# Two 512-column and 256-column matmuls in place of three 256-column ones in five weight products of a hybrid block

## The chip, the cores and the metric

One core of one Trainium2 chip runs the whole kernel. The metric is the device time of one execution in microseconds, as the median of several runs; smaller is better.

## The reference

Two transformer-like blocks run one after the other on 256 tokens of width 1024 (float32). Cut to what matters here:

```python
# block 1
proj = rms_norm(x, norm1_g) @ w_in            # q, k, v, conv_b, conv_c, conv_x, gate_a, gate_b
z    = conv_b * conv3(conv_c * conv_x)
mixed = sigmoid(gate_a) * (o_nsa @ w_branch_a) + sigmoid(gate_b) * (z @ w_branch_b)
x = x + mixed @ w_out
x = x + square(relu(rms_norm(x, norm2_g) @ w_up)) @ w_down      # 1024 -> 4096 -> 1024
# block 2: conformer convolution, top-k attention, cross attention, then
h = h + square(relu(rms_norm(h, norm_ffn_g) @ w_ff1)) @ w_ff2   # 1024 -> 4096 -> 1024
return rms_norm(h, norm_final_g)
```

`o_nsa` is the sum of three attentions (compressed, selected, window).

## The kernel before

Activations lie in SBUF with features on partitions and the 256 tokens along the free axis. Each matrix product takes its weights in units of 128x2048 values (four k-tiles of 128 rows times 512 output features). To keep float32 accuracy, weights and activations are each split into a high part (the value rounded to the matmul's input type) and a low part (the rest): `Stream.split` makes `wh` with a ScalarE copy (L123) and `wl` with a VectorE subtraction (L126) for every unit; activations are kept as `HL` tiles with a high and a low half. One product of a 128x128 weight block with a k-tile is then three matmuls of 256 moving columns into the same PSUM region: wh by the high activations (L264), wh by the low ones (L266), wl by the high ones (L268), in `mm3`. Low by low is left out. Where the text says a triple, it means these three.

`Feat` runs one group: 512 output features, as four feature tiles (`o` = 0 to 3) of 128. It takes two PSUM banks from the pool `psm` (four banks, handed out in turn): each bank holds two feature tiles of 256 columns. A group with 1024 input features has two chunks of one weight unit each, so 32 triples. In its last chunk it finishes the first bank (o = 0, 1; b = 0), hands it to the group's `evac` function, then the second (b = 1).

The order of the work on each engine is what the program's code gives on TensorE (its schedule is manual); on the other engines a scheduler orders the instructions when the program is built. Side work (attention, norms, convolution) is written as generators, and each `pump()` in a chunk advances them by one step, so their matmuls stand in TensorE's queue between the groups' matmuls. Every engine runs its own queue in order.

The places that matter below, in order of time:

- The six convolution groups. The last one is `ev_b`; its evacuation computes y from the convolution first (L813 on ScalarE; L814, L816, L819 on VectorE) and only then reads PSUM (L820).
- The four gate groups (`ev_g`, `ta` and `tb`), with `attention1` as side work: in each pump the scores of one chunk (L743 to L745), transposes of the chunk three steps earlier (L769) and, every second time, the products with v (L785).
- The two `ev_bb` groups (branch b), two `ba` groups (branch a), and the output projection.
- The first feed-forward: `ffn_up` with eight groups g = 0 to 7 (the first two interleaved, the rest one after the other), with `norm_side` as side work; then the down projection in `residual`, with two halves hf = 0, 1 of 32 k-tiles each. Its ev applies Relu on ScalarE (L929), squares on VectorE (L930) and splits (L396, L397).
- Block 2, at whose end stands the second `ffn_up` and a down projection of 512-column matmuls (`Tok`, L355 to L357: weights are the moving side there).

Of the kernel before, what the change touches and what calls it, by code (L numbers as in the profile page):

```python
# [9 lines left out]
F32 = mybir.dt.float32  # L10
F32R = mybir.dt.float32r
AF = mybir.ActivationFunctionType
ALU = mybir.AluOpType
# [3 lines left out]
T = 256  # L17
# [38 lines left out]
class Split:  # L56
# [11 lines left out]

    def lo(self, k, n=1):
        return self._part(1, k, n)  # L70

    def _part(self, h, k, n):
        t = self.tiles[k // 2]
# [87 lines left out]
def hybrid_conformer_kernel(ctx, tc, stop, dbg, xT, memT, wall, wtok, wkiwi, wcmp, par_d, cst_d, gfin_d, out):  # L161
# [27 lines left out]
    def S(shape, name, bufs=None, dt=F32):  # L189
        return sm.tile(shape, dt, name=name, tag=name, bufs=bufs) if bufs else sm.tile(shape, dt, name=name, tag=name)  # L190
# [16 lines left out]
    def turns(ap):  # L207

        return ap.rearrange("p (s a) -> p a s", s=2)

    def plain(ps):

        return ps.rearrange("p n (a s) -> p n s a", s=2)

    def v4(ap):
        return ap.rearrange("p n (s a) -> p n s a", s=2)
# [40 lines left out]

    ALL8 = list(range(8))

    def mm3(ps_ap, wh, wl, xh, xl, first, last, part=None):  # L260
        ps_ap = ps_ap.rearrange("p (a s) -> p a s", s=2)
        xh, xl = turns(xh), turns(xl)
        if part in (None, 0):
            P.matmul(out=ps_ap, lhsT=wh, rhs=xh, start=first, stop=False, skip_group_check=True)  # L264
        if part in (None, 1):
            P.matmul(out=ps_ap, lhsT=wh, rhs=xl, start=False, stop=False, skip_group_check=True)  # L266
        if part in (None, 2):
            P.matmul(out=ps_ap, lhsT=wl, rhs=xh, start=False, stop=last, skip_group_check=True)  # L268

    class Feat:  # L270


        def __init__(self, act, kts, evac, kmajor=False):
            self.act, self.kts, self.evac, self.kmajor = act, kts, evac, kmajor
            self.nch = len(kts) // 4
            self.ps = None

        def chunk(self, c):
            if self.ps is None:
                self.ps = [psm.tile([128, 2, T], F32, name="m", tag="m") for _ in range(2)]  # L280
            ps, act = self.ps, self.act
            wh, wl = W.next()
            wh = wh.rearrange("p (k o) -> p k o", k=4)
            if wl is not None:
                wl = wl.rearrange("p (k o) -> p k o", k=4)
            ks = self.kts[4 * c:4 * c + 4]
            end = c == self.nch - 1

            def one(kk, o, part=None):
                k = ks[kk]  # L290
                sl = slice(o * 128, o * 128 + 128)
                first = c == 0 and kk == 0 and o % 2 == 0
                last = end and kk == 3
                if wl is None:
                    P.matmul(out=plain(ps[o // 2])[:, o % 2], lhsT=wh[:, kk, sl], rhs=v3(act.raw(k)), start=first, stop=last, skip_group_check=True)  # L295
                else:
                    mm3(ps[o // 2][:, o % 2], wh[:, kk, sl], wl[:, kk, sl], act.hi(k), act.lo(k), first, last, part)

            if not end or self.kmajor:
                for kk in range(4):  # L300

                    for part in range(3) if self.kmajor and wl is not None else (None,):
                        for o in range(4):
                            one(kk, o, part)
                    if kk == 1:
                        pump()
                if end:
                    for b in range(2):
                        self.evac(plain(ps[b]), 2 * b, 2)
            else:  # L310
                for b in range(2):
                    for kk in range(4):
                        for o in (2 * b, 2 * b + 1):
                            one(kk, o)
                    self.evac(plain(ps[b]), 2 * b, 2)
                    if b == 0:
                        pump()
            pump()
# [56 lines left out]
    def prod(gs, pair=False):  # L375
        if pair:
            for c in range(gs[0].nch):
                for g in gs:
                    g.chunk(c)
        else:  # L380
            for g in gs:
                for c in range(g.nch):
                    g.chunk(c)

    def group(act, kts, evac, kmajor=False):
        prod([Feat(act, kts, evac, kmajor)])

    def tok_group(act, kts, n, evac):
        prod([Tok(act, kts, n, evac)])
# [93 lines left out]
    with tc.manual_schedule(engines=MANUAL):  # L483
# [344 lines left out]
        for dst in (ta, tb):  # L828
            for hf in range(2):
                def ev_g(ps, o, n):  # L830
                    d = dst[hf][:, o:o + n]
                    V.tensor_tensor(v4(d), ps, v4(bc(c1["rb"], n)), op=ALU.mult)
                    A.activation(out=d, in_=d, func=AF.Tanh, scale=0.5)

                group(xs, ALL8, ev_g)


        m1 = B8(name="m1")
        for hf in range(2):
            def ev_bb(ps, o, n):  # L840
                gated(m1[hf][:, o:o + n], tb[hf][:, o:o + n], ps)

            group(zs, ALL8, ev_bb)
        drain(at1)
        ms_ = HL("mh")

# [8 lines left out]

        prod([ba(0), ba(1)])

        def residual(act, kts, x, sp, gname, scale_b=None, kmajor=False, pair=True, stats=None):

            def one(hf):  # L860
                def ev(ps, o, n):
                    k = 4 * hf + o
                    if scale_b is None:
                        V.tensor_tensor(v4(at(x, k, n)), ps, v4(at(x, k, n)), op=ALU.add)
                    else:
                        t = S([128, 2, T], "pr", PR_BUFS)
                        V.tensor_tensor(v4(t), ps, v4(bc(scale_b, n)), op=ALU.mult)
                        V.tensor_tensor(at(x, k, n), t, at(x, k, n), op=ALU.add)
                    if sp is not None:
                        split_gain(sp, x, range(k, k + n), gname)  # L870
                    if stats is not None:
                        sq = S([128, 2, T], "pr", PR_BUFS)
                        A.activation(out=sq, in_=at(x, k, n), func=AF.Square)

                        if k == 0:
                            stats["sq"] = sq
                            return
                        acc = stats["sq"]
                        if k + n < 8:
                            V.tensor_tensor(acc, acc, sq, op=ALU.add)  # L880
                            if k + 2 * n == 8:
                                V.tensor_tensor(acc[:, 0], acc[:, 0], acc[:, 1], op=ALU.add)
                            return

                        def add_up():
                            stats["ps"] = col_stats(acc[:, 0], sq[:, 0], sq[:, 1])

                        later.append((STATS_LAG, add_up))

                return Feat(act, kts, ev, kmajor=kmajor and hf == 0)  # L890

            prod([one(0), one(1)], pair=pair)

# [4 lines left out]
        def ffn_up(act, src, tagr, bcast):  # L898
            res = {}

            def norm_side():
                for _ in range(9):
                    yield
                s = sq_sum(src, "s")
                for _ in range(5):
                    yield
                ps = col_stats(s)
                r = rstd_col(ps, D, "r" + tagr)
                r2 = const.tile([128, 2], F32, name="rsq" + tagr)
                V.tensor_tensor(r2, r, r, op=ALU.mult)  # L910
                res["col"] = r2
                if not bcast:
                    return
                dg = col_diag(r2)
                yield
                ps = diag_bcast(dg)
                rb = S([128, T], "rb", 4)
                A.activation(out=rb, in_=ps, func=AF.Copy)
                res["b"] = rb

            res["gen"] = start(norm_side())
            hs = Split([])
            gs = []
            for g in range(8):
                hs.tiles += HL("hh", 4).tiles

                def ev(ps, o, n, g=g):
                    r = S([128, 2, T], "pr", PR_BUFS)
                    A.activation(out=v4(r), in_=ps, func=AF.Relu)  # L929
                    V.tensor_tensor(r, r, r, op=ALU.mult)  # L930
                    split_into(hs, r, n, 4 * g + o)

                gs.append(Feat(act, ALL8, ev))
            prod(gs[:2], pair=True)
            prod(gs[2:])
            return hs, res
# [40 lines left out]
        mems, mem_steps, mem_sum = load_mem()  # L977
        msd = start(mem_side())
        st3 = {}
        residual(hs, list(range(32)), x, None, None, scale_b=res["b"], pair=False, stats=st3)  # L980
        drain(msd)
        dump2("x3", x)
        if stop == 1:
# [541 lines left out]
```

## Time and profile before

| what | value |
|---|---|
| median of 3 runs (lowest to highest) | 895.15 us (895.09 to 895.33) |
| the profiled execution's own time | 895.22 us |
| span of its trace, first to last instruction | 893.4 us |
| mean granted TensorE clock | 0.998 |

The trace gives spans from the first to the last instruction; 1.8 us of the execution's time lie outside it. A matmul's row shows its latency, which overlaps with the next one's; what a matmul takes from TensorE is read from the distance of two starts. "PE" is TensorE's matmuls, "PEld" its weight loads, "DVE" VectorE, "ACT" ScalarE, "POOL" GpSimd.

### The profile page before, as it was taken

The page shows a single profiled execution, that of the slowest core. Times are in us where ns is not written, and L with a number is a line of the kernel's source. Part 1 is how long each engine was busy: PE and PEld are TensorE (multiplying, and loading weights), DVE is VectorE, ACT ScalarE, POOL GpSimd, SP SyncE. Part 2 cuts the span into 40 slices and gives each one's busy share as a digit, 9 for nine tenths or more (in the row PEclk, how much of TensorE's full clock was granted, in tenths as well). Part 3 has the DMA queues.
Part 4 walks back from the last instruction along what each step waited for, and adds up shares of the span by engine and source line. Part 5 has one row for each costly group of instructions (what it writes and reads, how often), then busy time and mean ns, then how long its engine had stood idle before and what let it go on. Part 6 is the DMA issues. An engine that isn't in the chain of part 4 may idle for free.

```text
span 893.4 us, 17269 instructions
## 1 busy us (share of the span) xinstructions
PE 881.9 (99%) x7240; PEld 852.8 (95%) x7240; DVE 659.8 (74%) x1037; ACT 545.4 (61%) x925; POOL 18.6 (2%) x21
## 2 busy tenths in 40 slices
PE   9999999999999999999999999999999999999996
PEld 8999999999999999999998989999999999998885
DVE  6678899457787675648699999997787777665542
ACT  7634667444575564434697799977566657554432
POOL 0121000000000000000000000000000000000000
PEclk9999999999999999999999999999999999999999
DMA  8944623455555566554553356354565265555531
GB/s 305 313 161 146 222 98 140 158 211 198 190 190 189 192 241 219 197 189 140 186 209 107 139 193 236 112 192 166 199 250 203 104 216 189 190 202 209 198 142 48
DMA packets 25566, 165.01 MB, mean 185 GB/s; under 512 B 2960, under 2 KB 3600, under 8 KB 6928
## 3 DMA queue, kind: packets, MB, share of 16 engines
q1 hardware_dynamic: 25056, 163.37, 51.8%
q8 instruction: 57, 0.93, 0.4%
q10 hardware_dynamic: 432, 0.53, 0.2%
q14 instruction: 21, 0.17, 0.1%
HBM read 162.58 MB, written 1.05 MB: 183 GB/s over the span
## 4 chain that ended last, share of the span: by engine, by line
PE 89%; DVE 5%; ACT 2%; issue 1%; DMA 1%; POOL 1%; POOLq 0%; DVEq 0%
PE m L264 23%; PE m L266 23%; PE m L268 23%; PE m L355 4%; PE m L356 4%; PE m L357 4%; DVE wl L126 2%; PE m L295 2%; DMA wr<-in_wall_dram 1%; PE m L352 1%; DVE y L1147 1%; PE o L785 1%; PE s L769 1%; PE s L1065 1%; POOL coqk L631 1%
## 5 line engine op out<-in xcount | busy, mean ns | idle before, releaser
L126 DVE TENSOR_TENSOR wl<-wr,wh 128x1024 fp32r<-128x1024 f32 (+2 forms) x300 | 350.4, 1191 | 155.2 <-ACT wh L123 154.8
L123 ACT ACTIVATE wh<-wr 128x1024 fp32r<-128x1024 f32 (+2 forms) x300 | 298.5, 1028 | 204.2 <-PE m L266 95.9
L264 PE MATMUL m<-xnh,wh 128*128 128x256 f32 x376 | 106.6, 283 | 0.0
L266 PE MATMUL m<-xnh,wh 128*128 128x256 f32 x376 | 103.4, 275 | 0.0
L268 PE MATMUL m<-xnh,wl 128*128 128x256 f32 x376 | 103.4, 275 | 0.0
L264 PE MATMUL m<-xh,wh 128*128 128x256 f32 x384 | 100.5, 282 | 0.9 <-ACT xh L523 0.9
L266 PE MATMUL m<-xh,wh 128*128 128x256 f32 x384 | 98.0, 276 | 0.0
L268 PE MATMUL m<-xh,wl 128*128 128x256 f32 x384 | 97.8, 275 | 0.0
L1146 ACT ACTIVATE cp<-u,par 128x255 f32<-128x255 f32 (+23 forms) x192 | 78.8, 492 | 0.0
L266 PEld LDWEIGHTS m<-xnh,wh 128*128 128x128 f32 x376 | 72.2, 192 | 0.7 <-issue 0.5
L264 PEld LDWEIGHTS m<-xnh,wh 128*128 128x128 f32 x376 | 72.2, 192 | 0.7 <-issue 0.5
L264 PEld LDWEIGHTS m<-xh,wh 128*128 128x128 f32 x384 | 69.8, 192 | 2.8 <-issue 1.4
L268 PEld LDWEIGHTS m<-xnh,wl 128*128 128x128 f32 x376 | 72.2, 192 | 0.0
L264 PE MATMUL m<-x5h,wh 128*128 128x256 f32 x256 | 70.8, 277 | 0.0
L264 PE MATMUL m<-fh,wh 128*128 128x256 f32 x256 | 70.6, 276 | 0.0
L264 PE MATMUL m<-hh,wh 128*128 128x256 f32 x256 | 70.6, 276 | 0.0
L268 PE MATMUL m<-x5h,wl 128*128 128x256 f32 x256 | 70.4, 275 | 0.0
L266 PE MATMUL m<-fh,wh 128*128 128x256 f32 x256 | 70.4, 275 | 0.0
L268 PE MATMUL m<-fh,wl 128*128 128x256 f32 x256 | 70.4, 275 | 0.0
L266 PE MATMUL m<-hh,wh 128*128 128x256 f32 x256 | 70.4, 275 | 0.0
L268 PE MATMUL m<-hh,wl 128*128 128x256 f32 x256 | 70.4, 275 | 0.0
L266 PE MATMUL m<-x5h,wh 128*128 128x256 f32 x256 | 70.4, 275 | 0.0
(380 smaller groups left out, 2318.1 us busy)
## 6 DMA issues: line engine op xcount, KB each, us to landing
wr<-in_wall_dram SPq DMA_DIRECT2D x145, 1024.0 KB, 4.9
wr<-in_wall_dram SPq DMA_DIRECT2D x4, 512.0 KB, 9.1
mem<-in_memT_dram SPq DMA_DIRECT2D x4, 512.0 KB, 5.8
wr<-in_wtok_dram SPq DMA_DIRECT2D x2, 560.0 KB, 5.5
wr<-in_wall_dram SPq DMA_DIRECT2D x4, 256.0 KB, 5.1
wck<-in_wcmp_dram SPq DMA_DIRECT2D x2, 512.0 KB, 8.6
cst<-in_cst_dram SPq DMA_DIRECT2D x1, 776.0 KB, 10.7
x<-in_xT_dram SPq DMA_DIRECT2D x2, 256.0 KB, 4.2
```

What stands on the lines that cost most here:

```text
L123: self.nc.scalar.activation(out=hi[:, sl], in_=raw[:, sl], func=AF.Copy)
L126: self.nc.vector.tensor_sub(lo[:, sl], raw[:, sl], hi[:, sl].bitcast(F32))
L264: P.matmul(out=ps_ap, lhsT=wh, rhs=xh, start=first, stop=False, skip_group_check=True)
L266: P.matmul(out=ps_ap, lhsT=wh, rhs=xl, start=False, stop=False, skip_group_check=True)
L268: P.matmul(out=ps_ap, lhsT=wl, rhs=xh, start=False, stop=last, skip_group_check=True)
L295: P.matmul(out=plain(ps[o // 2])[:, o % 2], lhsT=wh[:, kk, sl], rhs=v3(act.raw(k)), start=first, stop=last, skip_group_check=True)
L352: P.matmul(out=o.rearrange("p a s -> p s a"), lhsT=act.raw(k)[:, tk], rhs=wh[:, w], start=first, stop=last)
L355: P.matmul(out=o, lhsT=xh, rhs=wh[:, w], start=first, stop=False)
L356: P.matmul(out=o, lhsT=xh, rhs=wl[:, w], start=False, stop=False)
L357: P.matmul(out=o, lhsT=xl, rhs=wh[:, w], start=False, stop=last)
L631: G.tensor_tensor(co, ms, mhalf, op=ALU.pow)
L1146: A.activation(out=p[:, i, 0:T - d], in_=u[hf][:, i, 0:T - d], func=AF.Copy, scale=w[i])
```

## The change

`Feat` gets a second form of chunk, used where `wide` is set. The high and the low activations of a k-tile are one moving side of 512 columns (`Split.both`), so that wh meets both in one matmul; wl by the high activations follows with 256 columns into the first half of the same bank. A feature tile now has a whole bank: its first half collects wh·high + wl·high, its second half wh·low. At the end ScalarE copies the second half to SBUF (into the pool `pr`, which attention uses too) and VectorE adds the first half to it; the group's `evac` then reads SBUF instead of PSUM. A wide group takes all four banks of `psm`, the first two when it starts and the other two after half of its first chunk.

Wide are the four gate groups, the two branch-b groups, groups 2 to 7 of both feed-forward up projections, and the first half of the first down projection. In the wide up groups Relu and square become one VectorE instruction.

```diff
+    def mm2(ps_ap, wh, wl, xhl, first, last):
+        P.matmul(out=ps_ap.rearrange("p h (a s) -> p h a s", s=2), lhsT=wh, rhs=xhl.rearrange("p h (s a) -> p h a s", s=2),
+                 start=first, stop=False, skip_group_check=True)
+        P.matmul(out=ps_ap[:, 0].rearrange("p (a s) -> p a s", s=2), lhsT=wl, rhs=turns(xhl[:, 0]), start=False, stop=last,
+                 skip_group_check=True)
...
+        def chunk_wide(self, c):
+            if self.ps is None:
+                self.ps = [None] * 4
...
+            for b in range(2):
+                for o in (2 * b, 2 * b + 1):
+                    if c == 0:
+                        self.ps[o] = psm.tile([128, 2, T], F32, name="m", tag="m")
+                for kk in range(4):
+                    for o in (2 * b, 2 * b + 1):
+                        sl = slice(o * 128, o * 128 + 128)
+                        mm2(self.ps[o], wh[:, kk, sl], wl[:, kk, sl], self.act.both(ks[kk]), c == 0 and kk == 0, end and kk == 3)
+                if end:
+                    t = S([128, 2, T], "pr", PR_BUFS)
+                    for i in range(2):
+                        m = self.ps[2 * b + i]
+                        A.activation(out=v4(t)[:, i], in_=plain(m)[:, 1], func=AF.Copy)
+                        V.tensor_tensor(v4(t)[:, i], plain(m)[:, 0], v4(t)[:, i], op=ALU.add)
+                    self.evac(v4(t), 2 * b, 2)
+                pump()
...
-                group(xs, ALL8, ev_g)
+                group(xs, ALL8, ev_g, wide=True)
...
-            group(zs, ALL8, ev_bb)
+            group(zs, ALL8, ev_bb, wide=True)
...
-                return Feat(act, kts, ev, kmajor=kmajor and hf == 0)
+                return Feat(act, kts, ev, kmajor=kmajor and hf == 0, wide=wide and hf == 0)
...
-                    A.activation(out=v4(r), in_=ps, func=AF.Relu)
-                    V.tensor_tensor(r, r, r, op=ALU.mult)
+                    if g < 2:
+                        A.activation(out=v4(r), in_=ps, func=AF.Relu)
+                        V.tensor_tensor(r, r, r, op=ALU.mult)
+                    else:
+                        V.scalar_tensor_tensor(out=v4(r), in0=ps, scalar=0.0, in1=ps, op0=ALU.max, op1=ALU.mult)
...
-                gs.append(Feat(act, ALL8, ev))
+                gs.append(Feat(act, ALL8, ev, wide=g > 1))
...
-        residual(hs, list(range(32)), x, None, None, scale_b=res["b"], pair=False, stats=st3)
+        residual(hs, list(range(32)), x, None, None, scale_b=res["b"], pair=False, stats=st3, wide=True)
```

**TensorE, first gate group.** Before, around the first pump of the first gate group: triples into the tile m_1587, the pump's scores (s_1620) and transposes (s_1635), then triples into m_1586 again.

```order
L264 MATMUL m_1587<-xh_128,wh_1356 128x256
L266 MATMUL m_1587<-xh_128,wh_1356 128x256
L268 MATMUL m_1587<-xh_128,wl_1357 128x256
L743 MATMUL s_1620<-kzh_312,qh_181 128x512
L744 MATMUL s_1620<-kzl_313,qh_181 128x512
L745 MATMUL s_1620<-kzh_312,ql_182 128x512
L769 MATMUL s_1635<-cst_80,pr_1434 128x128 x2
L264 MATMUL m_1586<-xh_129,wh_1356 128x256
```

The same place in the changed kernel, with the semaphores that an instruction waits on: pairs into m_1595, the pump, then the group's third and fourth PSUM tile, m_1632 and m_1633.

```order
L265 MATMUL m_1595<-xh_129,wh_1356 128x512
L267 MATMUL m_1595<-xh_129,wl_1357 128x256
L780 MATMUL s_1612<-kzh_312,qh_181 128x512 [waits DVE_49]
L781 MATMUL s_1612<-kzl_313,qh_181 128x512
L782 MATMUL s_1612<-kzh_312,ql_182 128x512
L806 MATMUL s_1627<-cst_80,pr_1434 128x128 [waits DVE_49]
L806 MATMUL s_1627<-cst_80,pr_1434 128x128
L265 MATMUL m_1632<-xh_128,wh_1356 128x512 [waits DVE_49]
L267 MATMUL m_1632<-xh_128,wl_1357 128x256
L265 MATMUL m_1633<-xh_128,wh_1356 128x512 [waits DVE_49]
```

The group takes two more banks after its first pump, and the first matmul into each of them waits for VectorE. Of four banks in turn, m_1632 and m_1633 are those that held the two tiles of the convolution group `ev_b` just before (m_1352 and m_1353).

**VectorE, the release of that bank.** Before: L820 with m_1353 is the last read of `ev_b`'s second bank; it stands between the attention's instructions (L747 to L758).

```order
L126 TENSOR_TENSOR wl_1591<-wr_1354,wh_1590 128x1024
L819 TENSOR_TENSOR y_1047<-y_1047,rb_427 128x512
L755 RECIPROCAL mx_1626<-mx_1626 128x2
L747 SCALAR_TENSOR_TENSOR pr_1668<-s_1664,cs__1203,cst_80 128x512
L756 TENSOR_TENSOR mx_1626<-mx_1626,gate_466 128x2
L820 TENSOR_TENSOR y_1047<-m_1353,y_1047 128x512
```

In the changed kernel (L857 is the former L820, L784 the former L747):

```order
L129 TENSOR_TENSOR wl_1589<-wr_1354,wh_1588 128x1024
L856 TENSOR_TENSOR y_1047<-y_1047,rb_427 128x512
L792 RECIPROCAL mx_1618<-mx_1618 128x2
L857 TENSOR_TENSOR y_1047<-m_1353,y_1047 128x512
L793 TENSOR_TENSOR mx_1618<-mx_1618,gate_466 128x2
```

The read of m_1353 has moved up by one large attention instruction and one tiny one; ahead of it VectorE's queue is the same as before.

**ScalarE, end of group g = 3 of the first feed-forward.** L307 are the copies of the second half banks (m_3223 and m_3224 are the third and fourth tile of the group), L955 the copy of the norm's broadcast, L433 the split of a finished tile.

```order
L307 ACTIVATE pr_3302<-m_3223 128x256
L126 ACTIVATE wh_3318<-wr_3197 128x1024
L955 ACTIVATE rb_3314<-s_3311 128x256
L126 ACTIVATE wh_3318<-wr_3197 128x1024
L433 ACTIVATE hh_2829<-pr_3270 128x512
L307 ACTIVATE pr_3302<-m_3224 128x256
```

Before, one Relu (L929) read this group's second bank after the two L123 and the L918 that correspond to L126 and L955; now the copy of m_3224 stands behind one more split (L433).

## Rows read from the trace of the kernel before

**Rows 1.** The page: busy us (share of span) and instructions of each engine.

```profile
PE 881.9 (99%) x7240; PEld 852.8 (95%) x7240; DVE 659.8 (74%) x1037; ACT 545.4 (61%) x925; POOL 18.6 (2%) x21
```

**Rows 2.** The longest wait of TensorE: total us, times, longest.

```profile
PE s L1164 <- DVE ys L1161: 1.1, 1, 1.1
```

**Rows 3.** Timeline of TensorE: first and last of three matmul runs (start, us).

```profile
177.87 0.28 PE L264 MATMUL m<-zh,wh 128*128 128x256 f32 x1
...
199.20 0.28 PE L268 MATMUL m<-zh,wl 128*128 128x256 f32 x1
...
803.53 0.38 PE L355 MATMUL m<-wh,hh 128*128 128x512 f32 x1
...
886.20 0.38 PE L357 MATMUL m<-wh,hh 128*128 128x512 f32 x1
...
30.56 0.28 PE L355 MATMUL m<-wh,xh 128*128 128x280 f32 x1
...
36.17 0.28 PE L357 MATMUL m<-wh,xh 128*128 128x280 f32 x1
```

**Rows 4.** Groups by line and shape: busy us, mean ns | idle before.

```profile
L727 ACT ACTIVATE pct<-s 128x256 f32<-128x256 f32 x1 | 0.4, 364 | 0.0
L221 DVE SCALAR_TENSOR_TENSOR m<-tb,m 128x256 f32<-128x256 f32 x8 | 3.0, 415 | 2.7 <-PE m L268 2.7
L929 ACT ACTIVATE pr<-m 128x512 f32<-128x512 f32 x32 | 18.8, 587 | 9.5 <-PE m L268 9.5
L400 DVE SCALAR_TENSOR_TENSOR mh<-m,mh 128x512 fp32r<-128x512 f32 x4 | 2.8, 690 | 0.7 <-ACT mh L399 0.7
```

**Rows 5.** Windows, core 0: length, busy us of each engine, granted clock.

```profile
114.00:125.00 11.00, 11.00 (x97) 10.46 (x96) 10.98 (x34) 6.17 (x18) 0.00 (x0) 1.00 0.28 97
125.00:136.00 11.00, 11.00 (x98) 10.16 (x97) 11.00 (x25) 8.38 (x21) 0.00 (x0) 1.00 0.47 159
```

**Rows 6.** Timeline of TensorE at the start of the first gate group.

```profile
117.76 0.38 PE L264 MATMUL m<-xh,wh 128*128 128x256 f32 x1
...
120.54 0.38 PE L743 MATMUL s<-kzh,qh 128*128 128x512 f32 x1
...
121.33 0.36 PE L264 MATMUL m<-xh,wh 128*128 128x256 f32 x1
```

**Rows 7.** Timeline of VectorE in the same stretch.

```profile
119.20 0.69 DVE L820 TENSOR_TENSOR y<-m,y 128x512 f32<-128x512 f32 x1
...
122.34 0.75 DVE L747 SCALAR_TENSOR_TENSOR pr<-s,cs__1203,cst 128x512 f32<-128x512 f32 x1
...
126.26 0.74 DVE L747 SCALAR_TENSOR_TENSOR pr<-s,cs__1203,cst 128x512 f32<-128x512 f32 x1
126.91 0.16 DVE L756 TENSOR_TENSOR mx<-mx,gate 128x2 f32<-128x2 f32 x1
126.97 0.69 DVE L820 TENSOR_TENSOR y<-m,y 128x512 f32<-128x512 f32 x1
```

**Rows 8.** Groups by line and shape on ScalarE and VectorE: busy us, mean ns | idle.

```profile
L123 ACT ACTIVATE wh<-wr 128x1024 fp32r<-128x1024 f32 x282 | 287.7, 1054 | 199.2 <-PE m L266 95.9 <-issue 58.7 <-PE m L357 32.4
L396 ACT ACTIVATE hh<-pr 128x512 fp32r<-128x512 f32 x32 | 20.2, 632 | 21.8 <-DVE pr L930 21.8
...
L397 DVE TENSOR_TENSOR hh<-pr,hh 128x512 fp32r<-128x512 f32 x32 | 22.0, 689 | 9.8 <-ACT hh L396 9.8
...
L126 DVE TENSOR_TENSOR wl<-wr,wh 128x1024 fp32r<-128x1024 f32 x282 | 338.1, 1222 | 147.4 <-ACT wh L123 147.1
```

**Rows 9.** Granted clock near the end (windows), and 128-column matmuls early and late (timeline).

```profile
889.00:890.00 1.00, 0.00 (x0) 0.00 (x0) 0.72 (x1) 0.69 (x1) 0.00 (x0) 0.92 0.00 0
890.00:891.00 1.00, 0.00 (x0) 0.00 (x0) 0.00 (x0) 0.00 (x0) 0.00 (x0) 0.50 0.38 152
...
0.98 5.45 PE L492 MATMUL m<-ones 128*128 128x128 f32 x26 [0.98 <-POOL mhalf L485]
...
274.80 0.61 PE L466 MATMUL s<-diag,ones 128*128 128x128 f32 x4
```

More of the change, by code (lines that the diff above doesn't have):

```diff
@@ L70, in lo, with both @@
         return self._part(1, k, n)
+    def both(self, k):
+        return self.tiles[k // 2][:, :, k % 2]
     def _part(self, h, k, n):
@@ L270, in hybrid_conformer_kernel, with __init__ @@
     class Feat:
-        def __init__(self, act, kts, evac, kmajor=False):
-            self.act, self.kts, self.evac, self.kmajor = act, kts, evac, kmajor
+        def __init__(self, act, kts, evac, kmajor=False, wide=False):
+            self.act, self.kts, self.evac, self.kmajor, self.wide = act, kts, evac, kmajor, wide
             self.nch = len(kts) // 4
             self.ps = None
+        def chunk_wide(self, c):
+            if self.ps is None:
+                self.ps = [None] * 4
+            wh, wl = (w.rearrange("p (k o) -> p k o", k=4) for w in W.next())
+            ks = self.kts[4 * c:4 * c + 4]
+            end = c == self.nch - 1
+            for b in range(2):
[14 more added lines that the diff above has]
+                pump()
         def chunk(self, c):
+            if self.wide:
+                self.chunk_wide(c)
+                return
             if self.ps is None:
@@ L383, in prod, with group @@
                     g.chunk(c)
-    def group(act, kts, evac, kmajor=False):
-        prod([Feat(act, kts, evac, kmajor)])
+    def group(act, kts, evac, kmajor=False, wide=False):
+        prod([Feat(act, kts, evac, kmajor, wide)])
     def tok_group(act, kts, n, evac):
@@ L856, in hybrid_conformer_kernel, with residual @@
         prod([ba(0), ba(1)])
-        def residual(act, kts, x, sp, gname, scale_b=None, kmajor=False, pair=True, stats=None):
+        def residual(act, kts, x, sp, gname, scale_b=None, kmajor=False, pair=True, stats=None, wide=False):
             def one(hf):
```

## The prediction

> **What bounds the kernel now.** I read the page's busy times first: the reader is to see that TensorE's matmuls fill 881.9 of 893.4 us, VectorE 659.8 and ScalarE 545.4 [rows 1]. The list of TensorE's waits is next: its longest is 1.1 us [rows 2]. So the end is set by the sum of the matmuls in TensorE's queue, and any new wait of TensorE comes on top of it in full. What a matmul takes from TensorE is the distance of two starts in a stretch where nothing else stands between them, not the 0.28 or 0.38 us of its row, which is latency. Last, windows and timelines of VectorE and ScalarE at the places where the order shows new waits: an engine at 74% over the span may be full for 20 us, and it is.
>
> **What the change takes away.** Triples become pairs: 32 in each of four gate groups, two branch-b groups and twelve up groups, and 128 in the first down projection, (4 + 2 + 12) x 32 + 128 = 704, so 704 matmuls fewer. Columns stay at 768. From rows 3, with the count of steps between the first and last start of each run: 256 columns 21.33 / 191 = 0.1117 us, 512 columns 82.67 / 383 = 0.2159, 280 columns 5.61 / 47 = 0.1194 [rows 3]. A triple is 3 x 0.1117 = 0.3350, a pair 0.2159 + 0.1117 = 0.3275. The saving is 7.5 ns a pair, 704 x 7.5 ns = **5.3 us**.
> Bounds: a line through 280 and 512 columns has 0.416 ns a column and 2.8 ns a matmul, and puts 256 columns at 0.1094, 2.3 ns below what they take. If the short matmul of a pair goes at 0.1094, since a long one lies ahead of it, the saving is 9.8 ns, 6.9 us. If the line's 2.8 ns is all that a matmul less gives back, 704 x 2.8 ns = 2.0 us. I take the measured distances, which the same two shapes show in long runs.
> The Trainium skill (TensorE: Matmul & The Clock Gate, section Back-to-back issue gap) has the gap of a warm matmul as columns / 2.4 GHz plus 2.5 ns, so by it a matmul less gives 2.5 ns, 1.8 us in all. The 512-column row fits it and the 256-column row is slower than it, which is where the difference lies.
>
> **What it adds beside TensorE.** 76 feature tiles (18 groups of four, and four of the down projection) each get a PSUM copy on ScalarE, by the nearest row 0.364 us, and an addition on VectorE, nearest row 0.415 [rows 4]: 27.7 and 31.5 us. In the wide up groups 24 Relus of 0.587 go from ScalarE (14.1 us), and 24 squares become one instruction of about 0.69 on VectorE [rows 4], which I count as no more than before. In all VectorE has some 32 us more, ScalarE 14. Both have over 230 us idle, so this costs nothing as a total; uncovered it is 0.78 us at a tile's end, where a next group wants the bank. All four banks belong to one group now, so two places matter.
>
> **The first gate group.** Its first pair stands where the first triple stood, at 117.76 [rows 6]. Eight triples and the queue's next instruction came at 120.54; eight pairs (2.62) and a start-up as before bring the pump to about 120.5, which lasts 121.33 - 120.54 = 0.79, to 121.3. Then the group's third bank is needed, the former bank of m_1352, which was read by 119.20 + 0.69 = 119.89 [rows 7]: no wait. One pair later, at 121.6, the fourth is needed, the former bank of m_1353. In the run before, its last read began at 126.97 [rows 7], since VectorE is full: 10.98 of 11.00 us busy, then 11.00 of 11.00 [rows 5]. Before the change nobody wanted that bank so soon. In the changed order this read has moved up by the large instruction at 126.26; what is ahead of it is as before, and the score products it needs are issued ahead of the stall. So it starts at 126.26, ends at 126.95, and TensorE stands from 121.6 to 126.95, **5.35 us**. Behind the waiting matmul stand all of TensorE's later ones, the next scores too, so VectorE then has fewer instructions released and works its backlog off; walking the three engines through the following gate and branch-b groups leaves me with no second wait of this kind. Bounds: 5.3, and 6.1 if a further large instruction (0.74) stays ahead of the read.
>
> **The clock.** At the end of the span TensorE's last matmul starts at 886.20 [rows 3], the granted clock is 0.92 in the microsecond from 889 and 0.50 in the next [rows 9]. So a TensorE that is idle for 3 to 4 us loses half its clock here (2.4 to 1.2 GHz), and the stall is longer. What it costs to get it back is bounded by the kernel's start: 26 matmuls of 128 columns take 5.45 us, 0.21 each, where later four take 0.61, at most 0.15 each, and 0.11 if the last one's latency of 0.28 is taken off [rows 3, 9]: 26 x 0.06 to 0.10, 1.5 to 2.6 us lost. From 0 (the clock holds) to 2.6, I take **1.5**, since the start also began after a much longer rest.
>
> **The first feed-forward, g = 3 to 4.** Here the copy of the group's last tile stands on ScalarE behind the other tile's copy, two weight splits, the norm's broadcast copy and one more split of a finished tile: 0.364 + 1.054 + 0.364 + 1.054 + 0.632, then its own 0.364 and VectorE's 0.415 [rows 4, 8], together 4.25 us after the group's last pair. The next group wants that bank after a pump of about 0.61 [rows 9], eight pairs (2.62) and one more (0.33): 3.56. TensorE waits some **0.7 us**. From 0 (if ScalarE has done a weight split earlier) to 1.8 (one more VectorE weight split, 1.222 [rows 8], ahead of the addition, in part). The other transitions, in both feed-forwards, the branch-b groups and the down projection, leave 0.1 to 1.2 us by the same walk, so I take 0 for them; if that is wrong it is rival 4.
>
> **Sum.** 895.22 - 5.3 + 5.35 + 0.7 + 1.5 = **897.5 us**, against the profiled execution's own 895.22 (893.4 of span and 1.8 around it). The median of the runs is 895.15, so 897.4 there; the difference is below all else here. 0.2% is 1.8 us, about what a measurement of this kernel can tell from no change: faster is below 893.4, slower above 896.9.
>
> **Rivals.**
> 1. The clock stays up. For it: the tail's fall is the only one seen, and the pump's matmuls lie close ahead of the stall. Then 895.22 - 5.3 + 5.35 + 0.7 = 896.0. Chance 0.25.
> 2. The other side: the bank is free in time. If VectorE reaches that read early, the 5.3 us stay in hand. For it: the read itself needs only a product that ended before 117.76 and y from three short instructions, so it is nothing but the order on VectorE that holds it. Against it: VectorE has no idle time there [rows 5]. Without the stall 895.22 - 5.3 + 0.7 = 890.6. It decides below a stall of 2.8 us (1.8 us of net gain), a read that ends by 124.4. Chance 0.17.
> 3. Only the fixed part is saved: 895.22 - 2.0 + 5.35 + 0.7 + 1.5 = 900.8. By the skill's 2.5 ns the sum would be 901.0. The traced 256-column distance speaks against it. Chance 0.05.
> 4. The late evacuation shows at more places: if ten other group ends in the up projections wait 0.7 us each, as at g = 3, 897.5 + 7 = 904.5. For it: margins of 0.1 us; against it: ScalarE's idle time. Chance 0.08.
>
> **How the numbers follow.** The forecast has the remaining 0.45. Its own range is 896.2 (clock loss 1.0, no feed-forward wait, 5.3 at the gate) to 899.1 (upward departures of 0.75, 1.1 and 0.8 taken as independent, 1.6 together). Rival 1 lies a little below it, rival 2 at 889 (6.9 saved) to 891.5. The range 889.5 to 900.0 holds the forecast, rival 1 and nearly all of rival 2, and leaves out rivals 3 and 4. Faster is rival 2, 0.17. Slower is rivals 3 and 4 and 0.34 of the forecast's 0.45 (the part above 896.9), 0.47; within 0.2% is the rest, 0.36.
>
> **What would show it.** In the changed kernel's list of TensorE's waits, one of about 5 us at L265 or L267 behind VectorE's L857, between 121.6 and 127; if it is missing, rival 2 holds. In windows behind it, from 125 to 132, a granted clock below 1.00; if 1.00, rival 1. In long stretches of pairs, starts 0.2159 and 0.1117 apart; if 0.221 and 0.1117, rival 3. In the first feed-forward one wait of TensorE on L308 below 1.5 us, and L307 near 0.36 us; if there are many, rival 4. The prediction fails if the order on VectorE runs ahead of my clocking, or if the pairs have a cost that no run of equal matmuls shows.

## The result and the profile after

The changed kernel takes **899.69 us** (median of 4 runs, 899.27 to 902.27) against 895.24 (4 runs) before: ratio 1.0053, 95% interval 1.0041 to 1.0065. It is slower by 4.4 us, half a per cent. The forecast was 897.5, slower, in a range from 889.5 to 900.0. The profiled execution took 899.43 us, 4.2 more than the profiled one of before; its span is 897.6.

In the rows below, L265 is the 512-column and L267 the 256-column matmul of a pair, L307 the copy of a half bank and L308 the addition, L857 the last read of `ev_b`'s bank (formerly L820), L126 and L129 the splits of weights (formerly L123 and L126), L433 and L434 those of finished tiles (formerly L396 and L397), L784 the large attention instruction (formerly L747).

The changed kernel's page, busy us and instructions:

```profile
PE 879.1 (98%) x6536; PEld 829.8 (92%) x6536; DVE 686.9 (77%) x1113; ACT 554.1 (62%) x977; POOL 17.9 (2%) x21
```

Against [rows 1] there are 704 matmuls fewer, VectorE has 27.1 us more, ScalarE 8.7 more. TensorE's busy time is only 2.8 us shorter, though 5.3 us of work are gone, and its idle time has grown from 11.5 to 18.5 us. The list of TensorE's waits (total us, times, longest) says where:

```profile
PE m L265 <- DVE y L857: 5.2, 1, 5.2
PE m L274 <- ACT xh L560: 1.4, 2, 0.9
PE m L265 <- DVE pr L308: 1.3, 1, 1.3
```

The first and the third are new; before, no wait was over 1.1 us [rows 2]; the second stands at the kernel's start (at 9.49 and 13.21 us), ahead of all that was changed. The timeline of TensorE at the first (start, duration, in us):

```profile
121.26 0.46 PE L265 MATMUL m<-xh,wh 128*128 128x512 f32 x1
121.56 0.27 PE L267 MATMUL m<-xh,wl 128*128 128x256 f32 x1
127.05 0.80 PE L265 MATMUL m<-xh,wh 128*128 128x512 f32 x1 [5.21 <-DVE y L857]
127.64 0.42 PE L267 MATMUL m<-xh,wl 128*128 128x256 f32 x1
127.85 0.63 PE L265 MATMUL m<-xh,wh 128*128 128x512 f32 x1
128.28 0.42 PE L267 MATMUL m<-xh,wl 128*128 128x256 f32 x1
...
131.01 0.38 PE L265 MATMUL m<-xh,wh 128*128 128x512 f32 x1
```

One pair into the third bank, then TensorE stands until 127.05. The six pairs behind it start 0.64 us apart, twice the usual, until 131.01. Windows of the same stretch (length, busy us of PE, PEld, DVE, ACT, POOL, then the granted clock):

```profile
121.00:124.00 3.00, 0.84 (x6) 0.47 (x4) 3.00 (x9) 0.76 (x3) 0.00 (x0) 1.00 0.00 0
124.00:126.00 2.00, 0.00 (x0) 0.00 (x0) 2.00 (x5) 1.09 (x4) 0.00 (x0) 0.53 0.00 0
126.00:128.00 2.00, 0.95 (x3) 0.86 (x4) 1.93 (x7) 0.63 (x1) 0.00 (x0) 0.50 0.61 135
128.00:130.00 2.00, 2.00 (x8) 1.73 (x7) 0.44 (x1) 0.00 (x0) 0.00 (x0) 0.50 0.92 389
...
131.00:132.00 1.00, 1.00 (x8) 0.85 (x7) 0.00 (x0) 0.57 (x1) 0.00 (x0) 1.00 0.00 0
```

The clock falls to half (1.2 of 2.4 GHz) at about 124.1, while TensorE still stands, and comes back at about 131, some 4 us after it has started again. VectorE meanwhile is full to the end of the stand, and its timeline shows the read that released the bank:

```profile
124.45 1.21 DVE L129 TENSOR_TENSOR wl<-wr,wh 128x1024 fp32r<-128x1024 f32 x1
...
126.30 0.69 DVE L857 TENSOR_TENSOR y<-m,y 128x512 f32<-128x512 f32 x1
```

Before, this read started at 126.97 [rows 7]; it is 0.67 us earlier, and nobody waited for it then.

How the loss builds up is seen from the first matmul of each stage in the two timelines:

| stage that starts | before | after | later by |
|---|---|---|---|
| gate groups | 117.76 | 117.75 | 0.0 |
| branch-b groups | 177.87 | 184.28 | 6.41 |
| first feed-forward, up | 231.47 | 237.42 | 5.95 |
| first feed-forward, down | 318.12 | 324.23 | 6.11 |
| block 2 | 404.78 | 409.92 | 5.14 |
| second feed-forward, up | 715.58 | 720.61 | 5.03 |
| second feed-forward, down | 803.53 | 807.71 | 4.18 |

Branch b and the first down projection, 64 and 128 pairs with no wait, gain 0.46 and 0.97 us: 7.2 and 7.6 ns a pair. The first up projection gains nothing. Its wait is at the fourth group's end, in the timelines of ScalarE, VectorE and TensorE:

```profile
282.74 0.62 ACT L433 ACTIVATE hh<-pr 128x512 fp32r<-128x512 f32 x1
283.26 0.38 ACT L307 ACTIVATE pr<-m 128x256 f32<-128x256 f32 x1
```

```profile
281.65 2.45 DVE L129 TENSOR_TENSOR wl<-wr,wh 128x1024 fp32r<-128x1024 f32 x2 [0.52 <-ACT wh L126]
284.02 0.68 DVE L434 TENSOR_TENSOR hh<-pr,hh 128x512 fp32r<-128x512 f32 x1
284.62 0.42 DVE L308 TENSOR_TENSOR pr<-m,pr 128x256 f32<-128x256 f32 x1
```

```profile
283.64 0.27 PE L267 MATMUL m<-fh,wl 128*128 128x256 f32 x1
285.18 0.45 PE L265 MATMUL m<-fh,wh 128*128 128x512 f32 x1 [1.27 <-DVE pr L308]
```

ScalarE's copy stands behind the splits as forecast and ends at 283.64, 0.11 us before TensorE wants the bank. But VectorE then still has a split of weights and one of a finished tile ahead of the addition, which starts only at 284.62. TensorE lost 285.18 - 283.64 - 0.11 = 1.43 us there, and 0.98 of it (284.62 - 283.64) is VectorE's queue.

The prices of the two, over all their groups (busy us, mean ns, idle before), are near the forecast's 0.364 and 0.415:

```profile
L308 DVE TENSOR_TENSOR pr<-m,pr 128x256 f32<-128x256 f32 x76 | 29.5, 416 | 5.0 <-ACT pr L307 4.9
L307 ACT ACTIVATE pr<-m 128x256 f32<-128x256 f32 x76 | 25.9, 378 | 21.5 <-PE m L267 21.5
```

### The profile page after: what moved, and what is told of

Its sections match the earlier page's. It is cut to its first block, busy times and chain, and to the rows that moved or that the text cites. A ratio compares the mean times of both kernels' runs of the same rounds, so it can differ in the third digit from the quotient of the medians.

```text
span 897.6 us, 15993 instructions
## 1 busy us (share of the span) xinstructions
PE 879.1 (98%) x6536; PEld 829.8 (92%) x6536; DVE 686.9 (77%) x1113; ACT 554.1 (62%) x977; POOL 17.9 (2%) x21
## 3 DMA queue, kind: packets, MB, share of 16 engines
HBM read 162.58 MB, written 1.05 MB: 182 GB/s over the span
## 4 chain that ended last, share of the span: by engine, by line
PE 75%; DVE 13%; ACT 7%; issue 3%; DMA 2%; POOL 1%; POOLq 0%; DVEq 0%; ACTq 0%
PE m L265 17%; PE m L274 12%; PE m L276 12%; PE m L278 12%; PE m L267 8%; DVE wl L129 5%; PE m L392 3%; PE m L393 3%; PE m L394 3%; ACT cp L1186 3%; DVE y L1187 2%; ACT wh L126 2%; DMA wr<-in_wall_dram 1%; DVE y L1190 1%; ACT pr L1144 1%
## 5 line engine op out<-in xcount | busy, mean ns | idle before, releaser
L129 DVE TENSOR_TENSOR wl<-wr,wh 128x1024 fp32r<-128x1024 f32 (+2 forms) x300 | 350.0, 1189 | 130.5 <-ACT wh L126 128.7
L126 ACT ACTIVATE wh<-wr 128x1024 fp32r<-128x1024 f32 (+2 forms) x300 | 297.9, 1029 | 176.9 <-issue 53.2
L274 PE MATMUL m<-xh,wh 128*128 128x256 f32 x256 | 64.1, 281 | 1.4 <-ACT xh L560 1.4
L265 PE MATMUL m<-fh,wh 128*128 128x512 f32 x192 | 63.4, 384 | 1.3 <-DVE pr L308 1.3
L265 PE MATMUL m<-x5h,wh 128*128 128x512 f32 x192 | 63.7, 385 | 0.1
L276 PE MATMUL m<-xh,wh 128*128 128x256 f32 x256 | 62.8, 276 | 0.0
L278 PE MATMUL m<-xh,wl 128*128 128x256 f32 x256 | 62.6, 275 | 0.0
L1187 DVE TENSOR_TENSOR y<-y,cp 128x1020 f32<-128x1020 f32 (+23 forms) x48 | 55.5, 1156 | 5.0 <-ACT cp L1186 3.7
L267 PE MATMUL m<-fh,wl 128*128 128x256 f32 x192 | 52.3, 273 | 0.0
L267 PE MATMUL m<-x5h,wl 128*128 128x256 f32 x192 | 52.3, 273 | 0.0
L265 PE MATMUL m<-xh,wh 128*128 128x512 f32 x128 | 45.8, 404 | 5.2 <-DVE y L857 5.2
L392 PE MATMUL m<-wh,hh 128*128 128x512 f32 x128 | 48.5, 379 | 0.0
L393 PE MATMUL m<-wl,hh 128*128 128x512 f32 x128 | 48.5, 379 | 0.0
L394 PE MATMUL m<-wh,hh 128*128 128x512 f32 x128 | 48.5, 379 | 0.0
L274 PEld LDWEIGHTS m<-xh,wh 128*128 128x128 f32 x256 | 45.2, 192 | 2.1 <-ACT xh L560 1.8
```

Of the source, the lines that this page charges most:

```text
L126: self.nc.scalar.activation(out=hi[:, sl], in_=raw[:, sl], func=AF.Copy)
L129: self.nc.vector.tensor_sub(lo[:, sl], raw[:, sl], hi[:, sl].bitcast(F32))
L265: P.matmul(out=ps_ap.rearrange("p h (a s) -> p h a s", s=2), lhsT=wh, rhs=xhl.rearrange("p h (s a) -> p h a s", s=2), start=first, stop=Fa ...
L267: P.matmul(out=ps_ap[:, 0].rearrange("p (a s) -> p a s", s=2), lhsT=wl, rhs=turns(xhl[:, 0]), start=False, stop=last, skip_group_check=True)
L392: P.matmul(out=o, lhsT=xh, rhs=wh[:, w], start=first, stop=False)
L393: P.matmul(out=o, lhsT=xh, rhs=wl[:, w], start=False, stop=False)
```

## The experiments

The comparisons are with the kernel before, which ran beside each of them on the same chip, at 895.4 to 895.5 us; the changed kernel's 899.7 was measured beside 895.24. The first gate group starts anywhere between 117.2 and 118.2 us in the profiled runs, so differences of a microsecond or less are checked by the length of the stage in the traces.

**The first gate group as triples.** If the stand comes from this group's wish for a fourth bank, two banks are enough.

```diff
-                group(xs, ALL8, ev_g, wide=True)
+                group(xs, ALL8, ev_g, wide=not (dst is ta and hf == 0))
```

> The first gate group goes back to triples; the other three gate groups stay pairs. Theory (TensorE stood 5.4 us because this group wanted a bank that VectorE had not yet read, and its clock fell for it): both costs go, 5.4 + 2.0 us (six pairs at 0.64 instead of 0.33), and 32 pairs' saving of 0.24 is given back: about 892.5, no wait of TensorE over 1.1 us near 121.6, granted clock 1.00 from 114 to 140. Rival (VectorE is full there, so the wait only moves on to the next wide group, whose banks the first gate group's evacuation frees late): one wait of 3 to 5 us near 137, 897 to 899.

Measured: 892.49 us, ratio 0.9966 (0.9953 to 0.9978): faster than before. In the windows TensorE is busy all the time at the full clock, and the second group's banks are free in time, though VectorE is as full as it was:

```profile
122.00:127.00 5.00, 5.00 (x46) 4.58 (x45) 5.00 (x12) 2.94 (x7) 0.00 (x0) 1.00 0.21 29
127.00:131.00 4.00, 4.00 (x36) 3.87 (x35) 4.00 (x12) 2.40 (x8) 0.00 (x0) 1.00 0.55 229
131.00:140.00 9.00, 9.00 (x64) 8.04 (x63) 9.00 (x22) 6.35 (x15) 0.00 (x0) 1.00 0.38 119
```

So this one stand and what followed it cost 899.7 - 892.5 = 7.2 us, more than all the pairs save. In the traces the four gate groups take 59.40 us, and 66.53 in the changed kernel, 7.1 less.

**The stand filled, wholly and by half.** 24 (then 12) matmuls whose result is overwritten stand ahead of the group's third feature tile. They change no result and let nothing start earlier. (The arguments are cut at the dots.)

```diff
+                if c == 0 and b == 1 and self.fill:
+                    for _ in range(self.fill):
+                        P.matmul(out=self.ps[2]..., lhsT=wh[:, 0, 256:384], rhs=self.act.both(ks[0])..., start=True, stop=False)
...
-                group(xs, ALL8, ev_g, wide=True)
+                gg = Feat(xs, ALL8, ev_g, wide=True)
+                gg.fill = 24 if dst is ta and hf == 0 else 0
+                prod([gg])
```

> 24 extra matmuls of 512 columns, whose result is overwritten, stand ahead of the first gate group's third feature tile: 5.18 us of work in the place where TensorE stood. Nothing else is changed, and the real work behind them cannot start earlier. Theory (the six slow pairs behind the stall are TensorE's clock, which fell because TensorE stood): the clock stays at 1.00, the pairs at 0.33, 2.0 us less, about 897.7. Rival (the pairs behind the stall are slow for another reason, late weights or the waits themselves): 899.7, with pairs of 0.64 or gaps at 127 to 131.

Measured: 897.80 us, 1.9 less than the changed kernel, by more work; the gate groups take 64.63 us instead of 66.53. TensorE's timeline (L302 are the 24) and the windows:

```profile
121.53 5.43 PE L302 MATMUL m<-xh,wh 128*128 128x512 f32 x24
...
127.75 0.38 PE L265 MATMUL m<-xh,wh 128*128 128x512 f32 x1
...
128.07 0.38 PE L265 MATMUL m<-xh,wh 128*128 128x512 f32 x1
```

```profile
124.00:126.00 2.00, 2.00 (x11) 1.76 (x10) 2.00 (x5) 1.09 (x4) 0.00 (x0) 1.00 0.00 0
126.00:128.00 2.00, 1.96 (x11) 1.51 (x10) 1.95 (x6) 0.63 (x1) 0.00 (x0) 1.00 0.46 82
```

The clock stays at 1.00 and the pairs behind start 0.32 us apart. The slow six pairs were the clock, and it did not fall where TensorE had work in place of the stand.

> 12 extra matmuls in place of 24 ahead of the third feature tile, so that TensorE stands some 2.7 us in place of 5.2; the stall ends at the same time. Theory (what the clock costs hangs on how long TensorE has stood: it holds over a shorter stand): 897.8, as with 24. Rival (any stand of some microseconds costs the six slow pairs): 899.7, with pairs of 0.64 from 127 to 131.

Measured: 897.80 us as well, the median of seven executions. In the timeline of the profiled one (897.59) TensorE stands half as long (L863 is L857 here), and the window that holds most of this stand has the full clock:

```profile
126.80 0.48 PE L265 MATMUL m<-xh,wh 128*128 128x512 f32 x1 [2.63 <-DVE y L863]
```

```profile
124.00:126.00 2.00, 0.17 (x2) 0.00 (x0) 2.00 (x5) 1.09 (x4) 0.00 (x0) 1.00 0.00 0
126.00:128.00 2.00, 1.20 (x7) 1.12 (x8) 1.93 (x7) 0.63 (x1) 0.00 (x0) 1.00 0.72 188
```

Here a stand of 2.6 us cost its own length and no more; the one of 5.2 cost 2.0 us on top. But only four of the seven executions are like this one (897.41 to 897.80, mean granted clock 0.999); the other three took 898.85 to 899.41 at a mean clock of 0.995 to 0.997, near the rival's 899.7. Where their clock was low no trace shows, so a stand of this length may cost more than its length. With 24 matmuls seven of eight executions lie from 897.22 to 898.25, and one at 899.01.

**The bank read first.** `ev_b` reads PSUM in its first VectorE instruction instead of its last; the number of instructions stays.

```diff
             def ev_b(ps, o, n):
+                t = S([128, 2, T], "yb", 1)
+                V.tensor_tensor(v4(t), ps, v4(bc(c1["rb"], n)), op=ALU.mult)
...
-                V.tensor_tensor(y_, y_, bc(c1["rb"], n), op=ALU.mult)
-                V.tensor_tensor(v4(y_), ps, v4(y_), op=ALU.mult)
+                V.tensor_tensor(y_, y_, t, op=ALU.mult)
```

> The last convolution groups' evacuation reads its PSUM bank first (bank times broadcast, into a tile of its own) and multiplies by y at the end, instead of reading the bank last; as many instructions as in the changed kernel. Theory (only the late read of that bank holds TensorE): the read ends before 123, the wait of 5.2 falls below 1.5, the clock holds, 892 to 893.5. Rival (VectorE is full and something else on it is late in its place): another wait of 3 us or more between 121 and 140, above 896.

Measured: 893.07 us, ratio 0.9973 (0.9963 to 0.9984). All four gate groups stay in pairs and the stand is gone. VectorE's timeline has the read of the second bank (L848 here) 6.6 us earlier than in the changed kernel, ahead of TensorE's wish:

```profile
119.72 0.68 DVE L848 TENSOR_TENSOR yb<-m,rb 128x512 f32<-128x512 f32 x1
```

Two short waits on L308, 0.38 and 0.40 us, appear at the start of the second gate group. So what was late was this read by its place in the queue; that VectorE is full was not by itself the cause.

**The wide tiles' evacuation first.** Copies and additions get a higher priority in the scheduler.

```diff
-                    for i in range(2):
-                        m = self.ps[2 * b + i]
-                        A.activation(out=v4(t)[:, i], in_=plain(m)[:, 1], func=AF.Copy)
-                        V.tensor_tensor(v4(t)[:, i], plain(m)[:, 0], v4(t)[:, i], op=ALU.add)
+                    with tc.high_priority(offset=URGENT):
+                        for i, m in enumerate(self.ps[2 * b:2 * b + 2]):
+                            A.activation(out=v4(t)[:, i], in_=plain(m)[:, 1], func=AF.Copy)
+                            V.tensor_tensor(v4(t)[:, i], plain(m)[:, 0], v4(t)[:, i], op=ALU.add)
```

> Copies and additions that empty the wide tiles' banks get a higher priority in the scheduler, so that in the feed-forwards they stand ahead of weight splits and of finished tiles' splits. Theory (the wait of 1.27 us in the first feed-forward, and two of 0.36 and 0.14 in the second, come from that order): they go, 1.6 us less, about 898.1; the wait of 5.2 us in the first gate group stays. Rival (ScalarE and VectorE are simply late there, and what is put back is missed elsewhere, weight splits first): new waits on L126 or L129, 899.5 or more.

Measured: 898.70 us (897.62 to 899.12), 1.0 less than the changed kernel, not 1.6; the profiled execution is the longest of the five. In the profiled runs the two up projections take 0.96 and 0.59 us less, as the waits on L308 are gone; the first has a new wait of 0.3 on the norm's diag (L497). The stand in the first gate group is the same 5.2 us, but the clock fell later and came back later, and the gate groups take 67.34 us instead of 66.53, 0.8 more. From 124 to 126 the clock is still at 0.98, where the changed kernel has 0.53; from 131 to 140 it is at 0.90 on average, where the changed kernel has 1.00:

```profile
124.00:126.00 2.00, 0.00 (x0) 0.00 (x0) 2.00 (x5) 1.09 (x4) 0.00 (x0) 0.98 0.00 0
131.00:140.00 9.00, 9.00 (x55) 7.84 (x54) 6.81 (x15) 4.69 (x12) 0.00 (x0) 0.90 0.23 61
```

**Both together.** First with the first gate group as triples, then with the bank read first and all pairs kept.

> Both together: the first gate group as triples, and the wide tiles' copies and additions with higher priority. Theory (two separate causes, so they add): 892.5 less what the second gave in the feed-forwards, 0.96 and 0.59, about 890.9; the wait on VectorE's diag (0.4 in the first feed-forward) stays. Rival (with the banks' emptying ahead of the attention on a full VectorE, the gate groups 2 to 4 wait for the attention instead): 892 or more, with waits between 131 and 178.

Measured: 891.07 us, ratio 0.9951 (0.9939 to 0.9964), as the theory has it. The gate groups take the same 59.40 us as without the priority, so they wait for nothing new.

> All four gate groups in pairs, with the convolution bank read first and the wide tiles' copies and additions first. Theory (both causes removed, no pair given up): 893.07 of the former alone, less the 1.55 of the latter in the feed-forwards, 891.5, and less 0.8 more if the two waits on L308 in the second gate group (0.38 and 0.40) go too: 890.7 to 891.5. Rival (on a VectorE full from 114 to 140 every instruction put ahead holds another back, so a wait in the gates takes back what is gained): 892 or more.

Measured: **890.52 us**, ratio 0.9943 (0.9931 to 0.9956), the fastest of all. Its list of TensorE's waits begins

```profile
PE s L1205 <- DVE ys L1202: 1.1, 1, 1.1
PE m L529 <- POOL mhalf L522: 1.0, 1, 1.0
```

and holds no wait on L308 or on `ev_b`. 895.47 - 890.52 = 4.95 us is nearly the whole of the 5.3 that 704 pairs were to save. Stage by stage, against the kernel before, the gate groups gain 0.96 us, branch b 0.47, the first down projection 0.97 and the second up projection 1.43, each 7.3 to 7.6 ns a pair. Only the first up projection falls short, with 0.80 us for 192 pairs that should give 1.44; TensorE waits 0.27 there for the norm's diag (L497), and what took the rest stays open.

**All gate groups as triples.**

```diff
-                group(xs, ALL8, ev_g, wide=True)
+                group(xs, ALL8, ev_g)
```

> All four gate groups as triples, the rest as changed. Theory (beyond the first group's stall a gate pair saves the same 7.5 ns as elsewhere): 96 pairs fewer than with only the first group as triples, 0.7 us more than its 892.5, 893.2. Rival (the additions on a full VectorE cost the gates what their pairs save): 892.5 or less.

Measured: 893.54 us, 1.05 more than with one group as triples (expected 0.7); the runs of this kernel alone lie from 892.59 to 894.62. The traces are sharper: the gate groups take 60.11 us here and 59.40 there, 0.71 more for 96 pairs, or 7.4 ns a pair. The gates' pairs are worth what pairs are worth elsewhere; with VectorE full, their copies and additions cost nothing there once no bank is awaited.

**Relu on ScalarE again.** On top of the first gate group as triples.

```diff
-                    if g < 2:
+                    if g < 8:
```

> First gate group as triples; in the wide up groups Relu on ScalarE and the square on VectorE are two instructions again, as before the change. Theory (this work reads SBUF and lies behind the banks' release, so it costs TensorE nothing): 892.5 within 0.5. Rival (14 us more on ScalarE put the next tiles' copies off, and the 1.3 us wait at the first feed-forward's fourth group grows and repeats): 894 or more.

Measured: 894.17 us, 1.7 more than 892.49. The theory was wrong. Between the two traces 1.42 us are the first up projection's (88.23 us against 86.81) and 0.5 the kernel's start; the second up projection takes 87.02 against 87.10. TensorE's waits have two on L308 instead of one:

```profile
PE m L265 <- DVE pr L308: 2.4, 2, 1.2
```

The timeline of ScalarE ahead of the new one, at the end of the first wide up group:

```profile
259.53 0.64 ACT L307 ACTIVATE pr<-m 128x256 f32<-128x256 f32 x2
262.49 0.63 ACT L967 ACTIVATE pr<-pr 128x512 f32<-128x512 f32 x1 [2.32 <-DVE pr L308]
263.03 0.37 ACT L307 ACTIVATE pr<-m 128x256 f32<-128x256 f32 x1
```

The Relu (L967) needs VectorE's addition, and ScalarE stands 2.32 us for it while the copy that helps to release the next bank (263.03) is queued behind it. With the one VectorE instruction the same copy ran as soon as TensorE had ended its tile:

```profile
261.53 0.38 ACT L307 ACTIVATE pr<-m 128x256 f32<-128x256 f32 x1 [1.89 <-PE m L267]
```

TensorE is 0.5 us behind here at that stage, so a whole microsecond is lost in the queue. The merged Relu and square are worth 1.4 us in the first up projection, and not by ScalarE's 14 us of work: they take a wait out of its queue.

**The second half of the first down projection too.**

```diff
-                return Feat(act, kts, ev, kmajor=kmajor and hf == 0, wide=wide and hf == 0)
+                return Feat(act, kts, ev, kmajor=kmajor and hf == 0, wide=wide)
```

> As with both together, and the second half of the first down projection in pairs too, 128 more. Theory (each pair saves 7.5 ns wherever the banks are free in time): 0.96 less, about 889.9. Rival (the second half's first tiles want the four banks that the first half has just filled, and their evacuation, copy, addition, scaling and residual, comes late): a wait of 1 us or more near the middle of the down projection, 891 or more.

Measured, on top of both together with the first gate group as triples: 896.64 us, 5.6 more than its 891.07, at a place that neither theory named. The down projection itself is 0.6 us shorter (0.96 expected). But its last tile is finished later. Two copies and two additions come ahead of its scaling (L904), behind a split of weights on each engine. VectorE's timeline has this scaling at

```profile
405.04 0.69 DVE L904 TENSOR_TENSOR pr<-pr,rb 128x512 f32<-128x512 f32 x1
```

and without this change, where the down projection ends within 0.02 us of the same time, at

```profile
402.27 0.68 DVE L904 TENSOR_TENSOR pr<-m,rb 128x512 f32<-128x512 f32 x1
```

The norm's statistics stand behind it and make TensorE wait. TensorE's timeline, and the windows:

```profile
406.12 0.38 PE L473 MATMUL s<-ones,pr 128*128 128x1 f32 x2 [1.83 <-DVE pr L919]
407.38 2.29 PE L473 MATMUL s<-ones,pr 128*128 128x1 f32 x10 [0.88 <-ACT pr L910]
```

```profile
404.00:406.00 2.00, 0.29 (x3) 0.10 (x1) 2.00 (x6) 0.61 (x1) 0.00 (x0) 1.00 0.04 12
406.00:408.00 2.00, 1.00 (x5) 0.92 (x6) 1.80 (x3) 0.63 (x1) 0.00 (x0) 0.74 0.00 0
408.00:410.00 2.00, 2.00 (x10) 2.00 (x11) 0.16 (x1) 0.00 (x0) 0.05 (x1) 0.50 0.55 127
```

Two waits of 1.8 and 0.9 us with two one-column matmuls between them, and the clock falls again; it is back at 1.00 from 414 on. The stage from 401.44 to 420.13 takes 18.69 us, where the kernel with both together takes 12.86.

## Why the prediction was right

**The saving.** Forecast 5.3 us, 7.5 ns a pair. In the changed kernel 128 pairs of the down projection run from 324.23 to 366.15, 41.92 / 128 = 0.3275 us each, the forecast sum of the two distances to the last digit:

```profile
324.23 0.38 PE L265 MATMUL m<-hh,wh 128*128 128x512 f32 x1
...
366.15 0.28 PE L274 MATMUL m<-hh,wh 128*128 128x256 f32 x1
```

Rival 3 falls with it. By the formula of the Trainium skill (TensorE: Matmul & The Clock Gate, section Back-to-back issue gap) a matmul less gives 2.5 ns; this trace has 7.5 ns. Why 256 columns take 2.3 ns more than the line through 280 and 512 was not tested and stays open.

**The stand in the first gate group.** Forecast 5.35 us, from 121.6 to 126.95 behind L857; measured 5.21 as the wait's row has it, and 5.38 by the starts (127.05 - 121.56, less 0.11). Place, releaser and time are as worked out from VectorE's timeline of before and the order. Rival 2 is out; reading the bank first showed that the place of the read in VectorE's queue was the cause.

**The clock.** Forecast 1.5 us within 0 to 2.6; measured 131.01 - 127.05 = 3.96 for six pairs, against 6 x 0.3275 = 1.97: 2.0 us. Filling the stand returned 1.9. Rival 1 is out. Two parts of the way there were not sound. The price was taken from the kernel's slow start, but the granted clock of before reads 1.00 there. So no row shows that start to be the clock, and that 1.5 came near 2.0 is in part luck:

```profile
2.00:3.00 1.00, 1.00 (x6) 1.00 (x6) 0.00 (x0) 0.65 (x2) 0.00 (x0) 1.00 0.57 147
```

And the 3 to 4 us of idle time before a fall came from the tail alone. In the changed kernel the clock fell some 2.3 us after the last matmul's end (at about 124.1), in the evacuation-first kernel some 4.0 after it.

**The first feed-forward's wait.** Forecast 0.7 within 0 to 1.8; measured 1.43. The place was right, and so was the cause in kind: the emptying of this bank stands behind splits. But the shares of the two engines were wrong. The forecast added up ScalarE's rows in full and had the copy end 3.83 us behind the group's last pair, but the rows overlap (behind the start of a weight split of 1.05 us the next instruction started after 0.95), and it ended some 3.3 behind it. Two thirds of the wait, 0.98 us, came from VectorE's queue instead: from one more weight split ahead of the addition, which the forecast had as the upper bound and did not take, and from the finished tile's low split (0.68), which it had left out.

**The other transitions.** Forecast 0, on margins of 0.1 to 1.2 us. The second up projection gains 0.85 where 192 pairs give 1.44, so 0.6 went, 0.5 of it in short waits behind pumps (side matmuls at 753.41 and 756.85, with the next pair 0.72 and 0.50 us behind instead of 0.36). With the evacuation first the whole 0.59 came back. Rival 4 was right in kind there, at less than a tenth of its 7 us. And the move of Relu to VectorE, to which the forecast gave no part in the time, is worth 1.4 us in the first up projection: there it is what kept these margins. In the second it made no difference (87.02 and 87.10 us).

**The work beside TensorE.** Forecast some 32 us more on VectorE and 14 on ScalarE, at no cost as a total; the pages show 27.1 and 8.7 more.

**The sum.** -5.3 + 5.4 + 2.0 + 1.4 + 0.6 = 4.1, against 4.2 between the two profiled executions. The forecast's +2.3 was small by 0.5 at the clock, 0.7 and 0.6 at the feed-forwards: the mechanisms hold, but for the shares of ScalarE and VectorE in the first feed-forward's wait, and three terms were too small, all in the same direction. The forecast's own range ended at 899.1, with 0.8 for the feed-forward where its stated bound gives 1.1 (1.8 - 0.7), so it should have been 899.2. The measured 899.7 lies above either, since the departures were taken as independent and all went one way. It lies inside the stated range by 0.3 us, which is luck: no term stands for that part of the range.

## What to carry to other kernels

On an engine that is busy all the time, a change that frees a few microseconds over hundreds of instructions can be undone by one bank that is read too late. When a group doubles the banks it holds, look up who read each of them last and where that read stands in its engine's queue; reading PSUM in the first instruction of a chain, and giving evacuations priority, turned a loss of 4.4 us into a gain of 5.0 here. The stand of TensorE had two prices here: its length, 5.4 us, and 2.0 us for the matmuls behind it at half the clock.

## What the runs showed of the hardware

The same stand of 5.2 us at the same place cost 2.0 us of slow matmuls in one profiled run and 0.8 more in another (the evacuation-first kernel), where the clock fell and came back some 1.8 us later. So what the clock takes is not fixed by the stand alone. One of the changed kernel's four executions took 902.27 us at a mean clock of 0.992, against 0.994 and 0.995 in the others.

A stand of 2.6 us left the clock at 1.00 in the profiled execution, and three of that kernel's seven executions ran longer at a lower mean clock. Waits of 1.8 and 0.9 us with two one-column matmuls between them brought it to 0.50.

24 matmuls whose result is thrown away made the kernel 1.9 us faster, and 12 of them did as much in four executions of seven.
